# Feed-forward weights split by two DMAs instead of ScalarE and VectorE, and one square moved from GpSimd to VectorE

## The chip, the cores and the metric

The kernel runs on one core of one Trainium2 chip. The metric is the device time of one execution in microseconds, the median of three runs. Times inside an execution come from one profiled execution and are counted from its first instruction.

## What is computed

Two layers of a decoder trunk over 512 tokens of width 1024. Each layer has a token mixer (pooling, latent attention and a recurrent unit, merged by gates, then an output projection `w_out`) and after it a feed-forward block with a hidden width of 4096. Only the feed-forward block is touched by the change:

```python
h = rms_norm(x, g_ffn[l])
x = x + jnp.square(jax.nn.relu(h @ w_ff1[l])) @ w_ff2[l]
```

All arrays are float32. The kernel keeps float32 accuracy on TensorE by splitting each operand into a high and a low part (type float32r) with high + low equal to the operand, and by summing three products: high by high, high by low, low by high.

## The kernel before

Activations lie transposed: 8 blocks of 128 channels by 512 tokens. Weights lie in DRAM as chunks of 128 by 1024 floats (512 KB), contraction on partitions. A chunk serves eight 128 by 128 blocks, and each block takes part in three matmuls of 512 columns (`three`), so a chunk is used by 24 matmuls.

`chunk` (line 132) brings a chunk in: SyncE's queue loads it into one of three `raw` buffers (`load`, line 127), ScalarE rounds it into the high part `whi` (line 137), and VectorE subtracts to get the low part `wlo` (line 138). `whi` and `wlo` have two buffers each. These buffers lie in the pool `wpool`, which is open for the whole program, and all chunks of both layers pass through them in order, those of the mixer and of the feed-forward block alike.

Per layer the program opens and closes pools of SBUF in nested blocks (lines 587 to 604). The pools `mix`, `at` and `mg` hold the mixer's tiles; `mg` holds the merged activations `mgh` and `mgl`, which are the moving operands of the output projection `wo` (lines 596 to 600), the last step of the mixer. When these pools are closed, the pool `ff` (`ffp` in the code) is opened at the place where they lay. The framework's rule for such a pool, in its default form that this kernel uses, is that all its tiles wait for every user of the closed pools on whose bytes it lies. The permanent pools take some 118 KB of a partition, `mix` and `at` together some 105 KB, and `ff` 72 KB (100 KB with the change), so `ff` cannot lie beside the mixer's pools.

The feed-forward block runs over two halves of the hidden width (line 605). A half has 16 chunks of `w_ff1`, one for each block of 128 hidden channels: 24 matmuls into an accumulator `f`, then `ft` = max(f, 0) times the norm's factor on VectorE (line 618), the high part `ah` = square of `ft` on ScalarE (line 621), the float32 square of `ft` in place on GpSimd (line 622), and the low part `al` on VectorE (line 623). Then come 16 chunks of `w_ff2`, two for each of the eight output blocks, 48 matmuls into one accumulator, which VectorE adds to x (line 523). That makes 64 chunks per layer and 128 in all. The order of instructions on each engine is set by the framework's scheduler when the program is built, by its own estimate of times and by program order.

Other work of GpSimd near the block: the sum of squares of x for the norms (line 168). SyncE's queue also stores and reloads x between the layers.

Of the kernel before, what the change touches and what calls it, by code (L numbers as in the profile page):

```python
# [10 lines left out]
F32R = mybir.dt.float32r  # L11
AF = mybir.ActivationFunctionType
# [3 lines left out]
P = 128  # L16
# [17 lines left out]
HALVES = 2  # L34
HEAD = 10           # matmuls of the second half of the tokens ahead of the first half's sum of squares
SPLIT = 4           # output blocks of the first half ahead of the second half's last addition
EARLY = (0, 2, 4, 6)  # heads that a gate is computed before
LRU_N = 9           # gates ahead of the gates of the LRU
DEPTH = 4           # column blocks of gates ahead of the merge
ON_POOL = 2         # heads from here on form their q on the Pool engine  # L40
N_X, N_TMP, N_E, N_Z, N_RAW, N_W = 15, 6, 5, 6, 3, 2
N_PSUM = dict(acc=3, s=2, t=2, o=1)
FB = FF // P // HALVES

# order of the weight chunks of a layer, each [128, 1024] with the contraction on partitions
C_CKV, C_KR, C_QL, C_LRU, C_POOL = 0, 2, 3, 6, 8
# [5 lines left out]

# columns of the per-channel vectors of a layer
V_GMIX, V_GQ, V_GKV, V_PSC, V_CW, V_CB = 0, 8, 11, 13, 15, 23
# [3 lines left out]

# columns of the constants
K_COS, K_SIN, K_MASK, K_ID, K_ONE, K_ROT, K_CNT, K_INV = 0, 512, 1024, 1536, 1664, 1792, 1920, 1952  # L60
# [4 lines left out]
def trunk(ctx: ExitStack, tc, x_in, wts, vecs, consts, out):  # L65
# [11 lines left out]

    # ---- constants and per-channel vectors
    cst = const.tile([P, NCONST], F32, name="cst")
# [13 lines left out]

    # blocks of x and gates share their buffers: x waits in DRAM while the branches are computed
    def xtile(name):
# [9 lines left out]

    # ---- helpers
    def acc(name, tag="acc", bufs=None):
# [24 lines left out]
    def chunk(l, c, cols=1024, off=0):  # L132
# [6 lines left out]
        return hi, lo  # L139

    def blk(t, k):
        return t[:, k * P:(k + 1) * P]

    def dense(dst, w, acts, off=0):
        """dst[m, t] = sum_k w[k, m] * act[k, t]"""
        terms = []
        for k, (h, lo_) in enumerate(acts):
            terms += three(blk(w[0], off + k), blk(w[1], off + k), h, lo_)
        matmuls(dst, terms)

    def split(src, hi, lo, scale=None, eng=nc.vector):
        """hi + lo = src * scale, each float32r"""
        if scale is None:
            nc.scalar.copy(hi, src)
            eng.tensor_tensor(lo, src, f(hi), op=ALU.subtract)
        else:
            nc.scalar.activation(hi, src, AF.Copy, scale=scale)
            nc.vector.scalar_tensor_tensor(lo, src, scale, f(hi), op0=ALU.mult, op1=ALU.subtract)  # L158
# [12 lines left out]
    def rsqrt_mean(s, n, dst, name):  # L171
        """dst = (sum over partitions of s / n + EPS) ** -0.5 on every partition"""
        h, lo = tmp(f"nh{name}", F32R), tmp(f"nl{name}", F32R)
        split(s, h, lo)
        tot = acc(f"tot{name}", "o", 1)
        matmuls(tot, [(ones, h), (ones, lo)])
        rsqrt(tot, n, dst, name)
# [27 lines left out]
    def setup():  # L205
        nc.scalar.dma_start(vec, vecs)
        nc.vector.memset(epst, EPS)
        nc.scalar.copy(warm, epst)
        nc.vector.memset(f(ones), 1.0)
        # the first two chunks come by halves, between the first blocks of x  # L210
        raws = [wpool.tile([P, 1024], F32, tag="raw", bufs=N_RAW, name=f"raw0_{c}") for c in range(2)]
        for k in range(KB):
            nc.sync.dma_start(x[k], x_in[k])
            if k < 4:
                c, cols = k // 2, slice(512 * (k % 2), 512 * (k % 2) + 512)
                nc.sync.dma_start(raws[c][:, cols], wts[0, c, :, cols])
        for c in range(2):
            hi, lo = ready[0, c] = wtiles(0, c)
            for i in range(2):
                cols = slice(512 * i, 512 * i + 512)  # L220
                nc.scalar.copy(hi[:, cols], raws[c][:, cols])
                nc.vector.tensor_tensor(lo[:, cols], raws[c][:, cols], f(hi[:, cols]), op=ALU.subtract)
        nc.sync.dma_start(cst, consts)
# [4 lines left out]
    def setup_vectors():  # L228
        for l in range(L):
            nc.vector.tensor_scalar(hb[:, l, :], vcol(l, V_BA, 28), 0.5, None, op0=ALU.mult)  # L230
        # sp4 = 4 * softplus(-lam), with log1p(z) = 2 * atanh(z / (2 + z))
        lam = const.tile([P, L, 2], F32, name="lam")
# [31 lines left out]
    def mixer(l, mix, rstd, xs):  # L264
        """pool, latent attention and RG-LRU branches; returns their inputs to the projections"""
        ot = [tuple(mix.tile([P, S], F32R, tag="ot", bufs=8, name=f"ot{l}_{p}{c}") for c in "hl") for p in range(4)]
        us = [mix.tile([P, S], F32, name=f"u{l}_{b}") for b in range(2)]
        with ExitStack() as st:
# [27 lines left out]

            # the first projections run while the norm of x is still being found
            a0, a1 = project(C_CKV, "s"), project(C_CKV + 1, "s")
# [4 lines left out]
            zc = [latent_in(a0, "ckv", 0), latent_in(a1, "ckv", 1)]  # L303
            # columns of the stationary: high and low part of the 32 columns, twice
            raw = load(l, C_KR)
# [35 lines left out]

            # multi-scale pooling: groups of 64 channels, windows 2 4 8 16
            def pool_in(b):
# [23 lines left out]

            # the "ssq" buffers are free from the latent norms to the norm of the ffn
            pm = [tmpp.tile([P, S], F32, tag="ssq", bufs=2, name=f"pm{l}_{b}") for b in range(2)]
# [5 lines left out]

            # ---- attention
            wv = chunk(l, C_V)
            v = []
            for t in range(4):
# [8 lines left out]
                v.append(vv)  # L388
            # the blocks (j, i), i >= j, of the transposed probabilities are at 3 j + i, and zeros at 11
            pt = [at.tile([P, 13, P], F32R, name=f"pt{l}{c}") for c in "hl"]  # L390
# [4 lines left out]
            for h in range(NH):  # L395
# [3 lines left out]
                if e == 0:  # L399
# [12 lines left out]
                    dense(qn, wq, qlat)  # L412
                # q: 64 rows as they are, 32 rows times cos, 32 rows times sin
                q = tmp(f"q{l}_{h}")
# [11 lines left out]
                for i in range(4):  # L426
# [3 lines left out]
                    p = at.tile([P, S + 8], F32, tag="e", bufs=N_E, name=f"p{l}_{h}{i}")  # L430
                    # p = -scale * (s + mask), its minimum is -scale * rowmax
                    nc.vector.tensor_tensor_reduce(
# [7 lines left out]
                for i in range(4):  # L440
# [5 lines left out]
                    split(tp[:, :n, :], *dst)  # L446
                # rows 0:64 and 64:128 of o are the products with the high and the low parts of v
                o = acc(f"o{l}_{h}", "o")
# [12 lines left out]
    def pool_lru_out(l, mix, us, pm):  # L461
        w = chunk(l, C_SMALL, 768)
        res = [], []
        for b in range(2):
# [6 lines left out]
            for g, t in enumerate((tr, ti)):  # L471
                a = acc(f"ra{l}_{b}{g}")
                dense(a, w, [ly], 2 * b + g)
                nc.scalar.activation(t, a, AF.Tanh, bias=hb[:, l, 2 * g + b:2 * g + b + 1], scale=0.5)
            # a = exp(-sp4 (1 + tr));  1 - a^2 = th (1 + a^2), th = tanh(sp4 (1 + tr))
            av, th = tmp(f"av{l}_{b}"), tmp(f"th{l}_{b}")
# [47 lines left out]

    # ---- final norm, the last block of x by halves of the tokens
    halves = [slice(0, S // 2), slice(S // 2, S)]
# [14 lines left out]
    def finish(k, accs, terms):  # L541
        """the last block of x and the final norm, by halves of the tokens"""
        ones32 = cst[:, K_ONE:K_ONE + P]
# [38 lines left out]

    # ---- program
    x = [xtile(f"x{k}") for k in range(KB)]
    saved = [x_in[k] for k in range(KB)]
    setup()
    for l in range(L):
# [15 lines left out]
        with ExitStack() as st:  # L603
            ffp = st.enter_context(tc.tile_pool(name=f"ff{l}", bufs=1))
            for hf in range(HALVES):
                base = C_FF + hf * FF_STEP
                act = []
                first = acc(f"f1{l}_{hf}0")
                dense(first, chunk(l, base), xs)
                if hf == 0:  # L610
                    norm_x(f"f{l}", rstd, ssq)
                for m in range(FB):
                    a = first
                    if m:
                        a = acc(f"f1{l}_{hf}{m}")
                        dense(a, chunk(l, base + m), xs)
                    t = tmp(f"ft{l}_{hf}{m}")
                    nc.vector.scalar_tensor_tensor(t, a, 0.0, rstd, op0=ALU.max, op1=ALU.mult)  # L618
                    h = ffp.tile([P, S], F32R, tag="ah", bufs=FB + 2, name=f"ah{l}_{hf}{m}")
                    lo = ffp.tile([P, S], F32R, tag="al", bufs=FB + 2, name=f"al{l}_{hf}{m}")  # L620
                    nc.scalar.activation(h, t, AF.Square)  # L621
                    nc.gpsimd.tensor_tensor(t, t, t, op=ALU.mult)  # L622
                    nc.vector.tensor_tensor(lo, t, f(h), op=ALU.subtract)
                    act.append((h, lo))
                for j in range(KB):
                    w = [chunk(l, base + FB + 2 * j + i) for i in range(2)]
                    final = l == L - 1 and hf == HALVES - 1
# [22 lines left out]
def _blocks(w):  # L650
    """[K, M] -> [M/128, 128, K]: per block of 128 columns, k-blocks side by side"""
    k, m = w.shape
# [69 lines left out]
def _constants():  # L722
# [9 lines left out]
    c[:, K_ONE:K_ONE + P] = 1.0  # L732
    # rows: twice cos * k, twice sin * k; columns: the rotated key, and its halves swapped with a sign
    half = ROPE // 2
# [34 lines left out]
```

## Time and profile before

| | us |
|---|---|
| median of three runs | 1408.69 (1407.93 to 1408.70) |
| span of the profiled execution | 1406.1 |
| TensorE busy | 1379.1 |
| VectorE, ScalarE, GpSimd busy | 773.8, 559.7, 320.7 |

The profiled execution's span runs from its first to its last instruction; the medians of the runs are 2.6 us above it. A busy TensorE counts pipelined matmuls from start to modelled end. Issuing a DMA isn't counted as busy time of an engine.

### The profile page before, as it was taken

What the parts mean: (1) busy time and instruction counts of PE and PEld (TensorE: products, weight loads), DVE (VectorE), ACT (ScalarE), POOL (GpSimd) and SP (SyncE); (2) the same over time, 40 slices, a digit from 0 to 9 for tenths busy, and PEclk for the clock granted to TensorE, in tenths of its full rate; (3) what the DMA queues carried; (4) which work ended last, traced back from release to release, by engine and by line L of the source; (5) the groups of instructions that cost most, each with busy time, mean ns of one, the idle gap of its engine ahead of it and who ended that gap; (6) DMA issues with size and microseconds to landing.
All of it is one profiled execution on the core that took longest, in us unless ns stands there. A gap on an engine that the chain in (4) does not pass through costs nothing.

```text
span 1406.1 us, 16117 instructions
## 1 busy us (share of the span) xinstructions
PE 1379.1 (98%) x6252; PEld 1142.1 (81%) x6252; DVE 773.8 (55%) x1122; ACT 559.7 (40%) x847; POOL 320.7 (23%) x234
## 2 busy tenths in 40 slices
PE   7999999999999999999999999999999999999997
PEld 5877888888888888888887878888888888888886
DVE  8978774574544234443368887655745433344323
ACT  5457683324332112323244777632333221232322
POOL 3265101132322002211115530111232200022112
PEclk9999999999999999999999999999999999999999
DMA  5321122253332323233332212223423233333231
GB/s 200 100 79 61 57 79 100 91 155 100 94 102 92 104 90 105 90 112 113 121 104 85 72 58 73 90 90 105 150 90 105 91 104 90 105 90 105 91 103 62
DMA packets 42124, 137.38 MB, mean 98 GB/s; under 512 B 4672, under 2 KB 6848, under 8 KB 42048
## 3 DMA queue, kind: packets, MB, share of 16 engines
q1 hardware_dynamic: 41328, 135.76, 30.6%
q8 instruction: 49, 0.80, 0.2%
q10 hardware_dynamic: 720, 0.59, 0.1%
q14 instruction: 27, 0.22, 0.0%
HBM read 132.14 MB, written 4.19 MB: 97 GB/s over the span
## 4 chain that ended last, share of the span: by engine, by line
PE 91%; DVE 6%; issue 1%; ACT 1%; DMA 0%; DVEq 0%; ACTq 0%
PE f L116 50%; PE ga L116 17%; PE wo L116 6%; PE pj L116 6%; PE in L116 5%; PE s L116 2%; PE o L452 1%; DVE wlo L138 1%; PE t L444 1%; DVE q L420 1%; PE qr L116 1%; PE ka L116 1%; PE qn L116 1%; DVE qll L158 1%; DVE p L438 0%
## 5 line engine op out<-in xcount | busy, mean ns | idle before, releaser
L137 ACT CAST whi<-raw 128x1024 fp32r<-128x1024 f32 (+1 forms) x236 | 246.7, 1045 | 687.4 <-issue 381.9
L138 DVE TENSOR_TENSOR wlo<-raw,whi 128x1024 fp32r<-128x1024 f32 (+1 forms) x236 | 307.0, 1301 | 162.3 <-ACT whi L137 162.2
L116 PE MATMUL f<-al,whi 128*128 128x512 f32 (+1 forms) x528 | 202.2, 383 | 0.0
L116 PE MATMUL f<-ah,whi 128*128 128x512 f32 (+1 forms) x528 | 202.0, 383 | 0.0
L116 PE MATMUL f<-ah,wlo 128*128 128x512 f32 (+1 forms) x528 | 202.0, 383 | 0.0
L116 PE MATMUL f<-xhf,whi 128*128 128x512 f32 x512 | 199.2, 389 | 0.0
L116 PE MATMUL f<-xlf,whi 128*128 128x512 f32 x512 | 199.2, 389 | 0.0
L116 PE MATMUL f<-xhf,wlo 128*128 128x512 f32 x512 | 199.2, 389 | 0.0
L622 POOL TENSOR_TENSOR ft<-ft 128x512 f32<-128x512 f32 x64 | 94.4, 1477 | 426.9 <-ACT ah L621 426.9
L116 PE MATMUL ga<-xhm,whi 128*128 128x512 f32 x384 | 151.3, 394 | 2.5 <-ACT q L415 2.5
L116 PE MATMUL ga<-xhm,wlo 128*128 128x512 f32 x384 | 151.2, 394 | 0.0
L116 PE MATMUL ga<-xlm,whi 128*128 128x512 f32 x384 | 150.6, 392 | 0.0
L116 PEld LDWEIGHTS f<-al,whi 128*128 128x128 f32 x528 | 99.2, 188 | 19.5
L116 PEld LDWEIGHTS f<-ah,wlo 128*128 128x128 f32 x528 | 99.2, 188 | 19.4
L116 PEld LDWEIGHTS f<-ah,whi 128*128 128x128 f32 x528 | 99.2, 188 | 19.2
L116 PEld LDWEIGHTS f<-xlf,whi 128*128 128x128 f32 x512 | 96.1, 188 | 20.0
L116 PEld LDWEIGHTS f<-xhf,wlo 128*128 128x128 f32 x512 | 96.1, 188 | 20.0
L116 PEld LDWEIGHTS f<-xhf,whi 128*128 128x128 f32 x512 | 96.1, 188 | 19.9
L618 DVE SCALAR_TENSOR_TENSOR ft<-f,rstdf 128x512 f32<-128x512 f32 x64 | 44.1, 692 | 102.1 <-PE f L116 102.0
L116 PEld LDWEIGHTS ga<-xhm,whi 128*128 128x128 f32 x384 | 72.2, 188 | 17.6 <-ACT q L415 3.0
L116 PEld LDWEIGHTS ga<-xlm,whi 128*128 128x128 f32 x384 | 72.2, 188 | 14.3
L116 PEld LDWEIGHTS ga<-xhm,wlo 128*128 128x128 f32 x384 | 72.2, 188 | 14.3
(366 smaller groups left out, 2119.8 us busy)
## 6 DMA issues: line engine op xcount, KB each, us to landing
raw<-wts SPq DMA_DIRECT2D x232, 512.0 KB, 3.5
x<-x_in SPq DMA_DIRECT2D x8, 256.0 KB, 5.4
xr<-x_in SPq DMA_DIRECT2D x8, 256.0 KB, 2.9
saved<-xr SPq DMA_DIRECT2D x8, 256.0 KB, 2.0
xr<-saved SPq DMA_DIRECT2D x8, 256.0 KB, 3.1
out<-xr SPq DMA_DIRECT2D x12, 128.0 KB, 1.8
raw<-wts SPq DMA_DIRECT2D x4, 320.0 KB, 2.9
raw<-wts SPq DMA_DIRECT2D x4, 256.0 KB, 4.5
```

What stands on the lines that cost most here:

```text
L116: ins = nc.tensor.matmul(dst, lhsT=a, rhs=b, start=(start and i == 0), stop=(stop and i == n - 1))
L137: nc.scalar.copy(hi[:, :cols], raw[:, :cols])
L138: nc.vector.tensor_tensor(lo[:, :cols], raw[:, :cols], f(hi[:, :cols]), op=ALU.subtract)
L158: nc.vector.scalar_tensor_tensor(lo, src, scale, f(hi), op0=ALU.mult, op1=ALU.subtract)
L420: eng.tensor_tensor(q[o:o + ROPE], qr[src], table[src], op=ALU.mult)
L444: nc.tensor.transpose(tp[:, j, :], blk(probs[i], j), ident)
L452: nc.tensor.matmul(o[:, q0 * P:], lhsT=v[j][:, h, :, :], rhs=pt[c][:, 3 * j + q0:3 * j + 4, :], start=(j == 0 and c == 0), stop=(j == 3 an ...
L618: nc.vector.scalar_tensor_tensor(t, a, 0.0, rstd, op0=ALU.max, op1=ALU.mult)
L622: nc.gpsimd.tensor_tensor(t, t, t, op=ALU.mult)
```

## The change

Feed-forward chunks no longer pass through `raw`, `whi` and `wlo`. A new function takes two tiles of the pool `ff`, with four buffers each (`fwh` and `fwl`). A DMA issued by GpSimd loads the chunk into `fwh`, casting from float32 to float32r. ScalarE writes its negative into `fwl`. A second DMA issued by GpSimd loads the same chunk from DRAM once more and adds it to what stands in `fwl`, which leaves the low part. The square of `ft` moves from GpSimd to VectorE, and `ah` and `al` go from 18 to 17 buffers. Comments and docstrings are dropped as well, which is left out here.

```diff
+N_FW = 4
+    def chunk_by_dma(l, c, pool):
+        hi, lo = (pool.tile([P, 1024], F32R, tag=t, bufs=N_FW, name=f"{t}{l}_{c}") for t in ("fwh", "fwl"))
+        nc.gpsimd.dma_start(hi, wts[l, c])
+        nc.scalar.activation(lo, f(hi), AF.Copy, scale=-1.0)
+        nc.gpsimd.dma_start(lo, wts[l, c], accum_op=ALU.add)
+        return hi, lo
...
-                dense(first, chunk(l, base), xs)
+                dense(first, chunk_by_dma(l, base, ffp), xs)
...
-                        dense(a, chunk(l, base + m), xs)
+                        dense(a, chunk_by_dma(l, base + m, ffp), xs)
...
-                    h = ffp.tile([P, S], F32R, tag="ah", bufs=FB + 2, name=f"ah{l}_{hf}{m}")
-                    lo = ffp.tile([P, S], F32R, tag="al", bufs=FB + 2, name=f"al{l}_{hf}{m}")
+                    h = ffp.tile([P, S], F32R, tag="ah", bufs=FB + 1, name=f"ah{l}_{hf}{m}")
+                    lo = ffp.tile([P, S], F32R, tag="al", bufs=FB + 1, name=f"al{l}_{hf}{m}")
                     nc.scalar.activation(h, t, AF.Square)
-                    nc.gpsimd.tensor_tensor(t, t, t, op=ALU.mult)
+                    nc.vector.tensor_tensor(t, t, t, op=ALU.mult)
                     nc.vector.tensor_tensor(lo, t, f(h), op=ALU.subtract)
...
-                    w = [chunk(l, base + FB + 2 * j + i) for i in range(2)]
+                    w = [chunk_by_dma(l, base + FB + 2 * j + i, ffp) for i in range(2)]
```

## Rows read from the trace of the kernel before

**Rows 1.** The page's parts 1 and 2: busy time by engine, and forty slices.

```profile
PE 1379.1 (98%) x6252; PEld 1142.1 (81%) x6252; DVE 773.8 (55%) x1122; ACT 559.7 (40%) x847; POOL 320.7 (23%) x234
PE   7999999999999999999999999999999999999997
```

**Rows 2.** The chain that ended last, in order of time: start us, length us, what.

```profile
311.69 43.52 PE wo L116 x192
355.21 8.61 PE f L116 x38
364.96 338.87 PE f L116 x1495
1001.30 43.52 PE wo L116 x192
1044.82 8.61 PE f L116 x38
```

**Rows 3.** Stretches: length, then busy time and count by engine, clock, DMA share, GB/s.

```profile
core 0: us, PE busy (x) PEld busy (x) DVE busy (x) ACT busy (x) POOL busy (x), PEclk, DMA share, GB/s
364.90:703.80 338.90, 338.90 (x1497) 280.62 (x1496) 137.59 (x152) 92.08 (x112) 58.12 (x38) 1.00 0.33 104
720.00:800.00 80.00, 77.96 (x351) 63.63 (x350) 68.08 (x98) 42.08 (x69) 34.87 (x27) 1.00 0.28 85
1054.50:1389.00 334.50, 334.50 (x1504) 278.10 (x1503) 132.16 (x145) 92.14 (x111) 57.20 (x38) 1.00 0.30 93
```

**Rows 4.** Groups of layer 0's feed-forward stretch: busy us, mean ns, idle before, releaser.

```profile
L137 ACT CAST whi<-raw 128x1024 fp32r<-128x1024 f32 x63 | 66.4, 1054 | 244.0 <-issue 138.8 <-PE f L116 105.3
L138 DVE TENSOR_TENSOR wlo<-raw,whi 128x1024 fp32r<-128x1024 f32 x63 | 77.2, 1225 | 71.8 <-ACT whi L137 71.8
L623 DVE TENSOR_TENSOR al<-ft,ah 128x512 fp32r<-128x512 f32 x32 | 23.0, 723 | 27.1 <-POOL ft L622 27.1
L622 POOL TENSOR_TENSOR ft<-ft 128x512 f32<-128x512 f32 x32 | 47.4, 1482 | 213.3 <-ACT ah L621 213.3
```

**Rows 5.** DMAs of the same stretch: queue, packets, MB, share; then issue to landing.

```profile
q1 hardware_dynamic: 10073, 34.87, 32.4%
raw<-wts SPq DMA_DIRECT2D x63, 512.0 KB, 3.5
```

**Rows 6.** Line 129 in 640 to 660 us, durations min/median/max in ns, of the issue.

```profile
L129 SPq DMA_DIRECT2D raw<-wts x4: 328/328/328, 640.7 to 657.1; - x4
```

**Rows 7.** Timeline of TensorE at the two ends of layer 0's and 1's `wo`.

```profile
311.30 0.39 PE L116 MATMUL pj<-ot_3h,wlo 128*128 128x512 f32 x1
...
1044.43 0.39 PE L116 MATMUL wo<-mgh,wlo 128*128 128x512 f32 x1
1044.66 0.39 PE L116 MATMUL f<-xhf,whi 128*128 128x512 f32 x1
```

**Rows 8.** Timelines of GpSimd and of VectorE where layer 1's mixer pools open.

```profile
703.89 0.11 POOL L345 MEMSET pz<- 128x8 f32 x1 [7.01 <-PE f L116]
...
703.86 0.69 DVE L523 TENSOR_TENSOR xr<-xr,f 128x512 f32<-128x512 f32 x1 [3.31 <-PE f L116]
704.50 0.08 DVE L333 MEMSET lz<- 128x8 f32 x2
704.55 0.17 DVE L392 MEMSET pt1h<- 128x128 f32 x1
```

**Rows 9.** TensorE's granted clock: stretches at the end, then matmuls of the start.

```profile
1396.00:1398.00 2.00, 0.70 (x2) 0.30 (x2) 0.82 (x3) 1.63 (x4) 0.00 (x0) 1.00 0.76 257
1398.00:1400.00 2.00, 0.00 (x0) 0.00 (x0) 1.77 (x5) 0.09 (x1) 0.58 (x1) 0.80 0.23 77
1400.00:1402.00 2.00, 0.00 (x0) 0.00 (x0) 2.00 (x3) 0.00 (x0) 2.00 (x3) 0.50 0.54 189
...
13.68 0.79 PE L116 MATMUL in<-xhm,wlo 128*128 128x512 f32 x1 [0.59 <-DVE wlo L222]
14.27 0.63 PE L116 MATMUL in<-xhm,whi 128*128 128x512 f32 x1
14.70 0.63 PE L116 MATMUL in<-xlm,whi 128*128 128x512 f32 x1
16.83 0.39 PE L116 MATMUL in<-xhm,whi 128*128 128x512 f32 x1
17.06 0.39 PE L116 MATMUL in<-xlm,whi 128*128 128x512 f32 x1
```

**Rows 10.** What SyncE's queue waited for: us in total, times, longest.

```profile
SPq L129 <- DVE wlo L138: 1026.3, 212, 10.5
```

## Prediction

> **What bounds the kernel now.** I read the busy shares first: TensorE is busy for 1379.1 of 1406.1 us, and its only lighter slices are the first and the last [rows 1]. Then the chain that ended last: the feed-forward blocks are long unbroken pieces of matmuls, 338.87 us for 1495 of them in layer 0, so one every 0.2267 us, and a chunk of 24 takes 5.44 us [rows 2]. Then the stretches: from 364.9 to 703.8 us TensorE is busy for all of 338.90 us, at the full clock, and in layer 1 for all of 334.50 us, while VectorE, ScalarE and GpSimd are busy for 137.6, 92.1 and 58.1 us of the first one [rows 3]. The reader is to see that in the block which the change touches no other engine sets the pace, and that there is no idle time of TensorE in it that a lighter VectorE or GpSimd could give back. Nor does the block wait at its door: the output projection `wo` ends at 355.21 us and the first feed-forward matmul starts at 355.21 us, and the same at 1044.82 us in layer 1 [rows 2]. The weights for it were converted during `wo`, because `whi` and `wlo` are always there, and SyncE's loads wait for a buffer (1026.3 us in 212 waits), not for the memory [rows 10].
>
> **What the change removes.** Per chunk it removes VectorE's subtraction of 1.225 us; ScalarE's rounding of 1.054 us becomes a negation of the same shape, which I take at the same time [rows 4]. GpSimd's square of 1.48 us becomes one on VectorE, whose nearest row is the subtraction of 0.72 us [rows 4]. So VectorE is at 64 x 1.225 - 32 x 0.72, some 55 us less per layer, and `al` is ready some 0.8 us earlier. All of it lies beside a TensorE that is busy all the time, so it is worth nothing. If that cover were gone (TensorE waiting for weights), it would still be worth nothing, since VectorE has slack. The 17th instead of the 18th buffer of `ah` and `al` costs nothing either: the second half needs its first new buffer when TensorE begins that half, and by then the first half's matmuls, in TensorE's own order, are done with theirs.
>
> **What it adds, in the steady state.** A chunk now needs two DMAs. The queue moved 34.87 MB in 32.4% of 338.9 us, which is 318 GB/s while it moves, or 1.65 us for 512 KB [rows 5]. The casting DMA I take at that. The adding DMA has to read what stands in `fwl` as well; I take it at twice, 3.30 us (low end 1.65, as a plain load; high end 6.6, if it runs at half speed). Together 4.95 us per 5.44 us: it fits, with little to spare. In time: a load took 3.5 us from issue to landing [rows 5]. From a free buffer to a ready chunk it is then 3.5 for the cast, 1.05 for the negation and 0.2 for the two handovers, and 3.5 + 1.65 for the addition, 9.9 us. Four buffers give 3 x 5.44 = 16.3 us. So the steady state holds with 6.4 us in reserve, at a cost of nothing. No row shows a DMA issued by GpSimd; the bounds of one issue are 0.33 us, SyncE's row [rows 6], and 1.5 us, about a whole GpSimd instruction on 512 columns [rows 4].
>
> The Trainium skill (DMA: Bandwidth & Descriptors, Latency and other measured facts) states about 1 us to the first byte for a DMA issued by GpSimd against 0.6 us for one from SyncE. By that page each DMA here would land 0.4 us later, and the sum below would grow by 0.8 us per layer; no run before shows it. The same page (Rules for kernel authors) says that an accumulating DMA reads its destination and writes it later. That speaks for the second read that I charge; without it the sum would shrink by 1.65 us per layer.
>
> **What it adds at the door of each block.** This is the term that counts. `fwh` and `fwl` are tiles of the pool `ff`, which lies where the mixer's pools lay, so the first cast has to wait for their last user, and that is the last matmul of `wo` at 355.2 us. The rows show that such a wait is real: when layer 1's mixer pools open where `ff` lay, a memset of GpSimd, which reads nothing, comes only at 703.89 us, after 7.01 us idle, released by the last feed-forward matmul; VectorE sat idle for 3.31 us up to 703.86 us, and its three memsets come after that too [rows 8]. In the kernel before, nothing at this door needs a tile of `ff` before the first accumulator is full, so the wait is hidden. After the change TensorE needs both parts of the first chunk. Its wait, from 355.2 us:
>
> - cast of chunk 0, issue to landing: 3.5 us [rows 5];
> - negation and two handovers: 1.05 + 0.2 = 1.25 us;
> - addition: 3.5 + 1.65 = 5.15 us;
> - queueing: casts 1 to 3 are issued right behind cast 0. Four casts of 1.65 us, from 1.85 us after the issue (3.5 - 1.65), are through after 8.45 us; the addition could start to move at 3.5 + 1.25 + 1.85 = 6.6 us, so it waits for 1.85 us;
> - less the two matmuls with the high part that run before the low part is needed: 2 x 0.2267 = 0.45 us.
>
> That is 11.3 us without work. TensorE's clock falls in such a gap: at the end of the program it was granted in full up to 1398 us, at 0.80 over the next 2 us and at 0.50 (1.2 GHz) after that, with the last matmul before 1398 us [rows 9]. At the start of the program seven matmuls from 13.68 to 16.83 us go at some 0.43 us each until the pitch is 0.23 us [rows 9]. I charge seven times 0.2 = 1.4 us. Behind that the next chunks follow: each addition takes 3.30 us of the DMA engines, the matmuls of a chunk 5.44 us. Sum per layer 12.7 us, two layers 25.4 us: a span of 1406.1 + 25.4 = 1431.5, and with the 2.6 us by which the median stands above the profiled span, **1434.1 us**. The bounds of this term per layer: 3.5 + 1.25 + 3.5 - 0.45 = 7.8 us, with no second read, no queueing and no slow clock; and some 21 us, if the addition moves at half speed (3.3 us more), each of two issues takes 1.5 us and the clock costs 3 us. That makes 1424 to 1451 us.
>
> What is late next: the mixer's first chunk in layer 1 no longer stands in one ring behind feed-forward chunks, so its conversion can be done earlier. The idle time of TensorE after that door is 80 - 77.96 = 2.0 us [rows 3], and that bounds the gain.
>
> **The rivals.**
>
> *No stall at the door (not slower).* If a tile of `ff` waited only for the users of its own bytes, `fwh` and `fwl`, the first tiles of the pool, would lie where `ot` and the latents lay, last read at 311.30 us [rows 7]. Then the 9.9 us chain would fit easily into the 43.5 us of `wo`. It decides if the first cast is issued before 345 us. The time would be 1408.7, or up to 2.0 us less by the door of layer 1's mixer: 1406.7 to 1408.7. Against it stand the framework's rule and the late memsets [rows 8].
>
> *GpSimd's order becomes the bound.* GpSimd works in order. If the scheduler put the addition of chunk c ahead of the cast of chunk c+1, that cast would be queued behind a wait for cast, landing and negation. One turn would then be 3.5 + 1.25 plus two issues: 5.4 us at 0.33 us per issue, no loss, and 7.75 us at 1.5 us, 2.3 us too long for each chunk. At 1 us per issue it is 6.75 us, 1.3 us too long; over some 120 chunks that is 157 us, a total of about 1590 us. For it: a landing plus a negation comes so close to 5.44 us that the order is a toss-up. Against it: with four buffers the next cast is free to go as soon as TensorE has left a buffer, which on a wait-free estimate is about when the addition is ready.
>
> *The DMA engines become the bound.* With the cast and the addition both at half speed, a chunk takes 3.3 + 6.6 = 9.9 us instead of 5.44 us, 4.5 us for each of some 124 chunks: about 1990 us. With the addition alone at half speed it is 8.25 us and about 1780 us. No row speaks for it but the 91% share worked out above, and none excludes it.
>
> **How the numbers follow.** The door stall with a steady state that holds: 0.48, 1434 us, own range 1424 to 1451. GpSimd's order or a longer chain that costs something in each chunk: 0.25, spread from 1450 to 1640. DMA engines too slow: 0.12, from 1600 up. No stall: 0.10, 1406.7 to 1408.7. Half a stall, where the first casts do get away early: 0.05, 1412 to 1424. From 1416 to 1640 us the first two cases, some of the third and most of the last lie inside, about 8 in 10. A measurement of this kernel tells 0.2%, 2.8 us, from no change. Faster by more than that needs more than the 2.0 us that the mixer's door holds: 0.03. The same: the rest of the no-stall case, 0.07. Slower: 0.90.
>
> **What would show it right or wrong.** Right: two idle gaps of TensorE, of 8 to 20 us each, just behind the last `wo` matmul of each layer, released by a DMA into `fwl`; the granted clock below 1.00 right after them; no idle time from then to the end of each block; the first cast on GpSimd's queue at the end of `wo`. Wrong in the door: a cast issued while `wo` is running. Wrong in the steady state: gaps once per chunk, at a DMA share near 1.0 (the DMA engines) or with GpSimd's queue waiting for ScalarE most of the time (the order). The forecast as a whole falls if the time is below 1420 or above 1455 us.

## The result, and the profile after

The changed kernel takes 1556.03 us (median; 1555.30 to 1559.03) against 1408.54 us before: a ratio of 1.105, 95% interval 1.1035 to 1.1064, or 147.5 us more. The forecast was 1434 us, with a range from 1416 to 1640 us. So the direction was right, the size was not, and the time that came out lies in the spread of the second rival, "GpSimd's order becomes the bound" (1450 to 1640 us).

First the stretches of the changed kernel, one for each mixer and each feed-forward block, in that order. Columns: stretch, length, busy time of TensorE, its weight loads, VectorE, ScalarE and GpSimd with counts, granted clock, DMA share, GB/s.

```profile
0.00:355.60 355.60, 342.23 (x1560) 281.56 (x1560) 251.38 (x419) 187.18 (x315) 102.87 (x80) 1.00 0.32 103
355.60:781.00 425.40, 375.44 (x1542) 299.06 (x1541) 84.87 (x126) 97.64 (x117) 101.64 (x136) 0.95 0.69 164
781.00:1121.90 340.90, 336.68 (x1560) 279.06 (x1558) 233.39 (x379) 173.06 (x291) 92.82 (x70) 1.00 0.27 85
1121.90:1554.80 432.90, 374.30 (x1594) 301.69 (x1594) 87.02 (x135) 101.22 (x124) 106.22 (x141) 0.95 0.68 160
```

The mixers are as they were (`wo` ended at 355.21 us before [rows 2]). The two feed-forward blocks hold the whole loss: 425.40 us instead of the 348.6 us from 355.2 to 703.8 us, and 432.90 instead of 361.3. In [rows 3] TensorE was busy without a gap at the full clock; now it is idle for 50.0 us of the first block (425.40 - 375.44) and needs 26.8 us more busy time for the same matmuls, at a mean granted clock of 0.95. GpSimd and ScalarE are busy for a quarter of the time, and the DMA engines for 0.69 of it: nothing that works is full.

Who waits, over the whole program (engine, line, what it waits for: us in total, times, longest):

```profile
POOL fwl L147 <- ACT fwl L146: 592.8, 122, 9.5
ACT fwl L146 <- DMA fwh<-wts: 389.6, 72, 8.7
PE f L117 <- DMA fwl<-wts: 86.8, 42, 3.5
POOL fwh L145 <- PE f L117: 19.7, 9, 6.3
```

The first line is the answer. GpSimd, which issues both DMAs, stands for 592.8 us in front of additions whose negation isn't done. It hardly ever waits for a free buffer (9 times), which is what it should be doing in a block that TensorE bounds. TensorE waits 42 times for a low part, about once in three chunks. GpSimd's timeline in the middle of the block shows why (start, length, engine, line, operation, count, idle time before and its releaser; L145 is the cast, L147 the addition):

```profile
469.74 0.90 POOL L145 DMA_DIRECT2D fwh<-wts  x1
478.58 0.88 POOL L147 DMA_DIRECT2D fwl<-wts  x1 [7.94 <-ACT fwl L146]
479.19 1.39 POOL L145 DMA_DIRECT2D fwh<-wts  x2
486.99 0.88 POOL L147 DMA_DIRECT2D fwl<-wts  x1 [6.42 <-ACT fwl L146]
488.28 0.89 POOL L147 DMA_DIRECT2D fwl<-wts  x1 [0.40 <-ACT fwl L146]
488.83 0.91 POOL L145 DMA_DIRECT2D fwh<-wts  x1
497.77 0.87 POOL L147 DMA_DIRECT2D fwl<-wts  x1 [8.04 <-ACT fwl L146]
```

Two turns alternate: one cast and its own addition, then two casts and their two additions. Each turn ends at an addition that stands right behind the casts and waits for the very cast just issued to land and be negated. The next cast stands behind it on the queue although its buffer is free. The two turns take three chunks through in 19.19 us (478.58 to 497.77), 6.40 us each, where TensorE needs 5.44. Over 128 chunks that is 123 us.

The length of a turn is mostly the cast's landing. The DMAs from 400 to 760 us (count, size, median us from issue to landing):

```profile
fwh<-wts POOLq DMA_DIRECT2D x56, 512.0 KB, 6.9
fwl<-wts POOLq DMA_DIRECT2D x55, 512.0 KB, 5.5
```

A cast lands after 6.9 us here, not after the 3.5 us that the prediction took from SyncE's loads; in these rows it is issued 0.6 us behind an addition (478.58 and 479.19 us).

The rest is the door. TensorE around the end of layer 0's `wo`:

```profile
355.46 0.39 PE L117 MATMUL wo<-mgh,wlo 128*128 128x512 f32 x1
360.37 0.77 PE L117 MATMUL f<-xhf,fwh 128*128 128x512 f32 x1 [4.52 <-DMA fwh<-wts]
...
368.73 0.79 PE L117 MATMUL f<-xhf,fwl 128*128 128x512 f32 x1 [3.22 <-DMA fwl<-wts]
```

The first matmul with a low part starts 13.0 us after `wo` (355.69 to 368.73), in layer 1 after 11.5 us, and it takes 0.79 us instead of 0.39 [rows 7]: the clock is at its lower level. GpSimd's side of it:

```profile
356.18 2.38 POOL L145 DMA_DIRECT2D fwh<-wts  x4 [1.80 <-PE wo L117]
...
361.67 0.92 POOL L147 DMA_DIRECT2D fwl<-wts  x1 [1.82 <-ACT fwl L146]
```

The first four casts are released by the last `wo` matmul, as the prediction said.

### The profile page after: what moved, and what is told of

The parts are those of the page before. It is cut to its first block, busy times and chain, and to the rows that moved or that the text cites. A ratio compares the mean times of both kernels' runs of the same rounds, so it can differ in the third digit from the quotient of the medians.

```text
span 1554.8 us, 16092 instructions
## 1 busy us (share of the span) xinstructions
PE 1428.7 (92%) x6252; PEld 1161.4 (75%) x6252; DVE 656.7 (42%) x1058; ACT 559.1 (36%) x847; POOL 403.6 (26%) x426
## 4 chain that ended last, share of the span: by engine, by line
PE 24%; issue 16%; DMA 7%; POOL 4%; DVE 3%; ACT 2%; DVEq 0%; POOLq 0%; ACTq 0%
PE ga L117 8%; PE f L117 5%; DMA fwh<-wts 5%; PE wo L117 3%; PE pj L117 3%; PE in L117 3%; DMA fwl<-wts 2%; POOL fwh L145 2%; POOL fwl L147 2%; ACT fwl L146 1%; PE s L117 1%; DVE wlo L139 1%; PE o L461 0%; PE t L453 0%; POOL ssqm L177 0%
## 5 line engine op out<-in xcount | busy, mean ns | idle before, releaser
L146 ACT ACTIVATE fwl<-fwh 128x1024 fp32r<-128x1024 f32 x128 | 135.4, 1058 | 585.6 <-DMA fwh<-wts 389.6
L147 POOL DMA_DIRECT2D fwl<-wts x128 | 113.0, 883 | 597.5 <-ACT fwl L146 592.8
L117 PE MATMUL f<-ah,fwl 128*128 128x512 f32 (+1 forms) x528 | 211.8, 401 | 44.8 <-DMA fwl<-wts 44.8
L117 PE MATMUL f<-xhf,fwl 128*128 128x512 f32 x512 | 207.9, 407 | 42.2 <-DMA fwl<-wts 42.0
L117 PE MATMUL f<-xhf,fwh 128*128 128x512 f32 x512 | 206.7, 404 | 10.2 <-DMA fwh<-wts 10.0
L117 PE MATMUL f<-al,fwh 128*128 128x512 f32 (+1 forms) x528 | 207.9, 394 | 1.0 <-DVE al L632 1.0
L117 PE MATMUL f<-ah,fwh 128*128 128x512 f32 (+1 forms) x528 | 208.5, 395 | 0.0
L117 PE MATMUL f<-xlf,fwh 128*128 128x512 f32 x512 | 205.8, 402 | 0.0
L138 ACT CAST whi<-raw 128x1024 fp32r<-128x1024 f32 (+2 forms) x108 | 111.7, 1034 | 196.8 <-issue 121.2
L139 DVE TENSOR_TENSOR wlo<-raw,whi 128x1024 fp32r<-128x1024 f32 (+2 forms) x108 | 150.2, 1391 | 19.1 <-ACT whi L138 18.7
L117 PEld LDWEIGHTS f<-xhf,fwh 128*128 128x128 f32 x512 | 100.4, 196 | 32.9 <-issue 12.7
L145 POOL DMA_DIRECT2D fwh<-wts x128 | 95.2, 786 | 24.7 <-PE f L117 19.7
```

The lines of the kernel that those rows point to most:

```text
L117: ins = nc.tensor.matmul(dst, lhsT=a, rhs=b, start=(start and i == 0), stop=(stop and i == n - 1))
L138: nc.scalar.copy(hi[:, :cols], raw[:, :cols])
L139: nc.vector.tensor_tensor(lo[:, :cols], raw[:, :cols], f(hi[:, :cols]), op=ALU.subtract)
L145: nc.gpsimd.dma_start(hi, wts[l, c])
L146: nc.scalar.activation(lo, f(hi), AF.Copy, scale=-1.0)
L147: nc.gpsimd.dma_start(lo, wts[l, c], accum_op=ALU.add)
```

## The experiments

Theory: GpSimd's queue, in the order in which the scheduler built it, costs some 120 us, and the door of the two blocks some 27 us. Rivals: the DMA engines or the memory are too slow for two transfers per chunk; the square on VectorE makes the low parts late.

### The order on GpSimd's queue

All of the change is kept, but each cast is put ahead of the addition of the chunk before it.

```diff
+        last = min(c + 1, NCH - 1)
+        for n in range(c, last + 1):
+            if (l, n) not in issued:
+                cast(l, n, pool)
...
-        nc.gpsimd.dma_start(lo, wts[l, c], accum_op=ALU.add)
+        with tc.issue_after(issued[l, last][1]):
+            nc.gpsimd.dma_start(lo, wts[l, c], accum_op=ALU.add)
```

> The changed kernel with GpSimd's queue put in the order cast of chunk c+1, then addition of chunk c, throughout. Theory A (GpSimd's queue order): in the changed kernel the queue stands 592.8 us in additions that wait for ScalarE's negation, with casts behind them whose buffers are free. With one cast always ahead, two chunks share one landing plus negation of about 8 us plus the issues of 0.9 and 0.6 us, so a chunk needs about 4.8 us, below TensorE's 5.44 us. The gaps per chunk go, the wait at the start of each block (some 13 us) stays: about 1435 us. Rival B (the DMA engines or their latency set the pace, whatever the order): nothing changes, 1545 to 1560 us.

Measured: 1436.60 us (1435.55 to 1438.91), ratio 1.0200, interval 1.0184 to 1.0215. The stretch from 400 to 760 us, columns as above:

```profile
400.00:760.00 360.00, 360.00 (x1590) 298.07 (x1589) 100.32 (x143) 102.12 (x124) 95.93 (x126) 1.00 0.83 181
```

The same two lines of the waits, and a piece of GpSimd's timeline (here L147 is the cast and L158 the addition):

```profile
POOL fwh L147 <- PE f L117: 402.4, 120, 10.0
...
POOL fwl L158 <- ACT fwl L156: 90.6, 100, 3.9
```

```profile
470.60 0.55 POOL L147 DMA_DIRECT2D fwh<-wts  x1 [3.17 <-PE f L117]
471.50 0.87 POOL L158 DMA_DIRECT2D fwl<-wts  x1 [0.35 <-issue]
476.04 0.55 POOL L147 DMA_DIRECT2D fwh<-wts  x1 [3.67 <-PE f L117]
477.34 0.89 POOL L158 DMA_DIRECT2D fwl<-wts  x1 [0.75 <-ACT fwl L156]
```

Not one instruction is added or taken away, and 119.4 of the 147.5 us are gone. TensorE is busy for 360.00 of 360 us. GpSimd's waits have changed over from ScalarE (592.8 to 90.6 us) to TensorE (19.7 to 402.4 us): it waits for free buffers, and TensorE waits for nothing. The DMA engines are busier than in the changed kernel (0.83 against 0.69; from 720 us on the stretch is already layer 1's mixer, and from 400 to 700 us the share is 0.93) and hold back nobody, so they were not the bound.

### The square back on GpSimd

In the changed kernel t*t goes back from VectorE to GpSimd.

```diff
-                    nc.vector.tensor_tensor(t, t, t, op=ALU.mult)
+                    nc.gpsimd.tensor_tensor(t, t, t, op=ALU.mult)
```

> The changed kernel with one part undone: t*t is on GpSimd again (32 squares of some 1.5 us per layer, in the first half-steps only). Theory A (GpSimd's queue, in order, sets the pace of the feed-forward block in the changed kernel): what is added to that queue is added to the time, unless it falls into its waits for ScalarE; 0 to 47 us per layer, so 1556 to 1650 us, and most likely 1575. Rival (the DMA engines or the memory set the pace): the square moves nothing, 1553 to 1559 us.

Measured: 1551.69 us (1548.35 to 1552.28), no time added, some 4 us less. That is below the theory's 1556 to 1650 us and just below the rival's 1553 to 1559 us, so this run doesn't tell the two apart. The theory in the form "what is added to that queue is added to the time" fell. What stood in its place is in the waits of this run:

```profile
POOL fwl L147 <- ACT fwl L146: 499.3, 102, 8.3
```

64 squares of 1.48 us [rows 4] are 94.7 us, and GpSimd's wait shrank by 93.5 us (592.8 to 499.3). The work fell into the waits. That fits a queue whose pace is set by the place of its waits and not by the amount of work on it; what shows it is the first experiment.

### The square alone

The kernel before, with only t*t on VectorE.

> The kernel before with the square of ft moved from GpSimd to VectorE and nothing else. The prediction's step: worth nothing, since TensorE is busy all through the blocks: 1408.5 us, within 1 us. A rival would be that VectorE, which also makes the low parts of the weights here, is late for TensorE: over 1412 us.

Measured: 1409.00 us (1408.00 to 1410.14), ratio 1.0000, interval 0.9991 to 1.0009. That part of the change is worth nothing, as the prediction had it.

### Each DMA alone

First only the high part by a casting DMA; the low part is a subtraction on VectorE from the chunk as SyncE loads it.

```diff
+        raw = load(l, c)
         nc.gpsimd.dma_start(hi, wts[l, c])
-        nc.scalar.activation(lo, f(hi), AF.Copy, scale=-1.0)
-        nc.gpsimd.dma_start(lo, wts[l, c], accum_op=ALU.add)
+        nc.vector.tensor_tensor(lo, raw, f(hi), op=ALU.subtract)
```

> Only the high part comes by the casting DMA; SyncE loads the chunk as before and VectorE subtracts for the low part, into fwl. GpSimd's queue then holds casts alone and waits for no negation. Theory A (queue order): no loss per chunk; at the start of each block the cast of 4.1 us and the subtraction of 1.2 us, less the two matmuls, and the slow clock: 6 to 7 us per layer, about 1421 us. Rival B (the casting DMA itself is too slow, 6.8 us to landing against 5.44 us per chunk): 1500 us or more.

Then only the low part by the adding DMA; ScalarE rounds and negates.

```diff
+        raw = load(l, c)
-        nc.gpsimd.dma_start(hi, wts[l, c])
+        nc.scalar.copy(hi, raw)
         nc.scalar.activation(lo, f(hi), AF.Copy, scale=-1.0)
         nc.gpsimd.dma_start(lo, wts[l, c], accum_op=ALU.add)
```

> Only the low part comes by the adding DMA; SyncE loads the chunk, ScalarE makes the high part and the negative. GpSimd's queue then holds additions alone. Theory A: a waiting addition holds up no cast, so no loss per chunk; at the start of each block the rounding and the negation of 1.05 us each and the addition of 5.6 us, less the two matmuls, and the slow clock: 8 to 9 us per layer, about 1425 us. Rival B (the adding DMA itself is too slow): 1500 us or more.

Measured: the cast alone 1422.90 us (1421.98 to 1423.92), the addition alone 1434.87 us (1433.00 to 1436.04). In both, TensorE is busy for 300.00 us from 400 to 700 us: neither DMA costs anything in the steady state, and what is lost lies at the doors. With the cast alone that is 7.2 us per layer (a landing of 4.04 us and one subtraction). With the addition alone it is 13.2 us, 10 us in all more than I expected: the addition stood on GpSimd behind the last addition of the sum of squares (L177), and TensorE waited for the norm as well (9.4 us in two waits for `nhf`):

```profile
359.86 1.27 POOL L177 TENSOR_TENSOR ssqf<-ssqf,sqf 128x512 f32<-128x512 f32 x1 [6.26 <-ACT sqf L176]
361.07 2.81 POOL L147 DMA_DIRECT2D fwl<-wts  x3
```

The two runs also give each transfer's price, since GpSimd's DMA queue holds 128 transfers of one kind (packets, MB, share of 16 engines). The cast, in a span of 1420.3 us, and the addition, in 1431.2 us:

```profile
q0 software_dynamic: 18432, 67.12, 15.3%
```

```profile
q0 software_dynamic: 18432, 67.12, 28.5%
```

0.153 x 1420.3 / 128 = 1.70 us for a cast and 0.285 x 1431.2 / 128 = 3.19 us for an addition, 4.89 us for both. The prediction had taken 1.65, 3.30 and 4.95.

### Three buffers instead of four

The run with the order changed, and N_FW = 3.

> The kernel with the queue in order (one cast ahead) and three buffers instead of four. There a cast took 5.1 us and an addition 6.9 us to land, with the negation and the issues some 14 us from a free buffer to a ready chunk; three buffers give 2 x 5.44 = 10.9 us. So the time should rise by 0.6 us (with the shorter landings of less loaded queues) to 1.8 us per chunk, to 1500 to 1650 us. If the reserve were as large as the prediction had it (9.9 us needed), it would stay at 1437 us.

Measured: 1555.64 us (1552.18 and 1559.11), 119 us more than with four, some 0.95 us for each of 125 chunks. So in this order the reserve of four buffers is less than one chunk's 5.44 us, not 6.4. It is not a clean measure of the landings: in this order the addition of a chunk also waits behind a cast that waits for a buffer, and with three buffers only one chunk's time is left from there, against a landing of 6.3 us. How much of the 0.95 us each of the two makes wasn't separated. The waits of this run are a warning for the reading above:

```profile
POOL fwh L147 <- PE f L117: 590.6, 122, 10.6
...
PE f L117 <- DMA fwl<-wts: 88.2, 76, 2.7
```

GpSimd waits for free buffers even more than with four (590.6 against 402.4 us), and yet the block is late: here the buffers come free too late. That nothing is lost is seen in TensorE's own waits, not in GpSimd's.

### The door: which bar holds the first casts

Expected from the prediction: the pool's rule holds the first cast until the end of `wo`. First the rule is relaxed, in the changed kernel and in the one with the order changed.

```diff
-            ffp = st.enter_context(tc.tile_pool(name=f"ff{l}", bufs=1))
+            ffp = st.enter_context(tc.tile_pool(name=f"ff{l}", bufs=1, reuse_waits="tile"))
```

> The changed kernel with the pool ff waiting only for users of its tiles' own bytes, so that the first four casts may be issued while the output projection runs. Both theories: the wait at the start of each block goes (TensorE began the first low-part matmul 13.1 us after the end of wo in layer 0, 11.5 us in layer 1), the loss per chunk stays: 1556 - 25 = about 1531 us. If the rival that said the pool's rule costs nothing were right, it would stay at 1556 us.

> Both edits: the queue order with one cast ahead, and the pool that waits by bytes. Theory A: nothing of the loss is left, 1408 to 1412 us. Rival B: 1525 to 1535 us, as with the pool's edit alone.

Measured: 1551.81 us (1548.62 to 1559.34) and 1431.60 us (1429.18 to 1432.81): 4 and 5 us better than without it, not 25; the first of the two differences is smaller than the spread of its own runs. GpSimd's timeline of the second one:

```profile
353.89 1.78 POOL L188 TENSOR_TENSOR ssqf<-ssqf,sqf 128x512 f32<-128x512 f32 x1 [3.66 <-ACT sqf L187]
355.62 2.37 POOL L147 DMA_DIRECT2D fwh<-wts  x4
```

The casts wait for nothing now and still go out at 355.6 us: the scheduler had put them on the queue behind the sums of squares, each of which waits for a chunk of `wo`. A second bar stood where the first was taken away. Next, the first four casts are put ahead of the sums of squares.

```diff
+            for c in range(N_FW):
+                cast(l, C_FF + c, ffp)
             xs = gained(l, V_GFF, f"f{l}")
-            rstd, ssq = rstd_tile(f"f{l}"), sumsq_x(f"f{l}")
+            with tc.issue_after(issued[l, C_FF + N_FW - 1][1]):
+                rstd, ssq = rstd_tile(f"f{l}"), sumsq_x(f"f{l}")
```

> Both edits of the run before, and GpSimd's queue is made to hold the first four casts of a block ahead of the additions for the sum of squares of x (line 177), behind which they stood until 355.6 us. Theory (the wait at the start of each block has two bars, the pool's rule and GpSimd's queue order; only both together free it): the casts go out at about 311 us, when the last matmul on ot has run, the first chunks are ready during wo, and nothing is left of the loss: 1408 to 1413 us. Rival (the additions for the norm, now behind casts and additions of weights, come late, or early transfers collide with wo's loads): 1420 us or more.

Measured: 1431.89 us (1431.31 to 1434.47), nothing gained. GpSimd, then ScalarE:

```profile
313.60 2.37 POOL L147 DMA_DIRECT2D fwh<-wts  x4 [3.40 <-PE pj L117]
...
359.79 0.92 POOL L158 DMA_DIRECT2D fwl<-wts  x1 [31.44 <-ACT fwl L156]
```

```profile
356.87 1.05 ACT L138 CAST whi<-raw 128x1024 fp32r<-128x1024 f32 x1 [3.25 <-issue]
357.82 0.72 ACT L177 ACTIVATE xhf<-xr,vec 128x512 fp32r<-128x512 f32 x1
358.44 1.99 ACT L156 ACTIVATE fwl<-fwh 128x1024 fp32r<-128x1024 f32 x2
```

The casts are 42 us earlier, and the addition isn't: the negation stands on ScalarE behind work that follows the last chunks of `wo`. That is a third bar. The next run puts the casts, negations and additions of the first three chunks ahead of the norm on both engines, and the fifth chunk's cast behind the sums of squares.

```diff
+            for c in range(N_FW - 1):
+                chunk_by_dma(l, C_FF + c, ffp)
+            _, neg, add = made[l, C_FF + N_FW - 2]
+            with tc.issue_after(neg), tc.issue_after(add):
+                xs = gained(l, V_GFF, f"f{l}")
+                rstd, ssq = rstd_tile(f"f{l}"), sumsq_x(f"f{l}")
```

> Everything of the change stays; the pool waits by tile, each cast stands ahead of the addition of the chunk before it, and the casts, negations and additions of a block's first three chunks stand on GpSimd and ScalarE ahead of the norm's sums of squares and ahead of whi and xhf of the last output-projection chunks. Theory A (the stall at the door has three bars one behind the other, the pool's rule, GpSimd's order and ScalarE's order, so that freeing one or two of them moves nothing): all three are free now, TensorE goes from wo to f without a gap over 2 us, and the time is 1408 to 1413 us, level with the kernel before. Rival (the stall has a further cause that the order doesn't remove, such as the moving operand xhf or the weights of the last wo chunks coming late): a gap of 5 us or more stays at each door, and the time is 1420 us or more.

Measured: 1437.90 us (1436.45 to 1439.41), 6 us worse than the run before, and the theory's number missed. ScalarE:

```profile
357.31 1.04 ACT L138 CAST whi<-raw 128x1024 fp32r<-128x1024 f32 x1 [4.38 <-PE wo L117]
358.26 2.94 ACT L162 ACTIVATE fwl<-fwh 128x1024 fp32r<-128x1024 f32 x3
361.12 4.99 ACT L184 ACTIVATE xhf<-xr,vec 128x512 fp32r<-128x512 f32 x8
```

The negations now stand ahead of `xhf` but still behind the last rounding of `whi`, which waits for a matmul of `wo`; and all of `xhf` has become late too. So this run had not removed the third bar. The next one goes round ScalarE: GpSimd, idle from 316 us on, negates the first three chunks, and `gained` is left where it was.

```diff
+        if C_FF <= c < C_FF + N_FW - 1:
+            neg = nc.gpsimd.tensor_scalar(lo, f(hi), -1.0, None, op0=ALU.mult).ins
+        else:
+            neg = nc.scalar.activation(lo, f(hi), AF.Copy, scale=-1.0).ins
```

> Like the run with three bars, but the negations of a block's first three chunks are made by GpSimd instead of ScalarE, and whi, xhf and xlf are left where the changed kernel has them; only the norm's sums of squares on GpSimd stand behind the three additions. In the run with three bars the negations still came at 358.26 us, because they stood on ScalarE behind the rounding of the last chunk loaded during wo, which waits for a matmul of wo until 357.31 us; GpSimd has nothing else to do from 316 to 355 us. Theory A (the third bar is ScalarE's order, and that run didn't remove it): the first additions are issued by about 335 us, both parts of the first chunk are there before wo ends, the gap of TensorE at each door is under 3 us, and the time is 1408 to 1414 us. Rival 1 (the negation or the addition waits for the end of wo itself, because fwl lies on bytes that wo still reads): the additions are issued only after 355 us and 1425 to 1435 us come out. Rival 2 (the norm comes late instead, because its sums of squares now stand behind the additions): a gap at the first ft and 1415 to 1425 us.

Measured: 1423.52 us (1422.12 to 1423.79), above the theory's 1408 to 1414 us and in the range of rival 2. The additions go out at 326.56 us, and the first `f` matmul follows the last `wo` matmul without a gap. One gap is left in each block; TensorE and ScalarE there:

```profile
373.73 0.39 PE L117 MATMUL f<-xhf,fwl 128*128 128x512 f32 x1
378.71 0.79 PE L117 MATMUL f<-xhf,fwh 128*128 128x512 f32 x1 [4.59 <-DVE ft L652]
```

```profile
368.12 1.06 ACT L165 ACTIVATE fwl<-fwh 128x1024 fp32r<-128x1024 f32 x1 [5.87 <-DMA fwh<-wts]
...
372.12 0.69 ACT L211 ACTIVATE nyf<-totf,epst 128x512 f32<-128x512 f32 x1 [1.64 <-PE totf L117]
374.37 1.06 ACT L165 ACTIVATE fwl<-fwh 128x1024 fp32r<-128x1024 f32 x1 [1.56 <-DMA fwh<-wts]
375.33 0.61 ACT L212 ACTIVATE ntf<-nyf 128x512 f32<-128x512 f32 x1
```

The norm's factor is late, not because of the sums of squares (rival 2 as I had put it) but because its step `ntf` stands behind a negation that waits for a landing: a fourth bar, of the same kind. The last run puts `totf` earlier on TensorE and the fifth chunk's negation behind `ntf`.

```diff
+            with tc.issue_after(norm["ntf"]) if c == C_FF + N_FW else ExitStack():
+                neg = nc.scalar.activation(lo, f(hi), AF.Copy, scale=-1.0).ins
...
+                            matmuls(a, ts[:6], stop=False)
+                            with tc.issue_after(norm["tot"]):
+                                matmuls(a, ts[6:], start=False)
```

> Like the run in which GpSimd makes the first three negations, which left one gap of TensorE in each block, 4.6 us long at 373.9 us, before the matmul that waits for ft. In that run the norm's factor came late: the two matmuls of totf stood at 370.79 and 371.69 us, and its ntf on ScalarE at 375.33 us behind a negation that waited for a cast to land. Here the totf matmuls stand in the second chunk of the block, and the negation of the fifth chunk stands behind ntf. Theory A (the rest of the loss is the fourth bar, the norm's steps queued behind a negation): ntf is done by about 366 us, the gap is gone, and the time is 1408 to 1412 us, within 0.3% of the kernel before. Rival (the fifth chunk's low part comes late now, because its negation and addition are put back): a gap of 3 to 6 us at the fifth chunk, and 1415 to 1424 us.

Measured: 1412.06 us (1410.39 to 1413.01), ratio 1.0019, interval 1.0010 to 1.0029. TensorE's one remaining wait for something of this block, then two pieces of the chain that ended last (start, length, what):

```profile
PE f L117 <- DVE ft L663: 1.4, 1, 1.4
```

```profile
314.07 43.52 PE wo L117 x192
357.59 12.41 PE f L117 x54
```

The gap in layer 0 is gone and that in layer 1 is 1.4 us. `totf` came only at 369.83 us, later than I had meant; it was early enough. Which of the two edits closed the gap wasn't separated. By the medians 3.2 us of the loss are left. The profiled execution is 4.8 us longer than the one before (spans of 1410.9 and 1406.1 us), and 2.4 us of that are there before `wo` begins (314.07 against 311.69 [rows 2]): in the first 20 us TensorE runs at the lower clock until 18.7 us instead of 16.8 [rows 9], ahead of everything the change touches. That part isn't shown to be the change's, since in the run with the square alone, whose time is level, `wo` began at 313.49 us. From the start of `wo` to the end the execution is 2.4 us longer, of which 1.4 are the gap in layer 1.

No version beats the kernel before. With all bars away the change comes within 0.2% of it, which is what [rows 3] said: there was no idle time of TensorE in the block to win.

## Why the prediction was right or wrong

- *What bounds the kernel*: right. TensorE had no gap in the block; the best form of the change comes out within 0.2%, and the square on VectorE is worth 0.0%.
- *Steady state*: this is the step that failed: "the steady state holds with 6.4 us in reserve, at a cost of nothing". It lost 119 us. The sum added up landings as if each cast were issued when its buffer came free. That holds only if nothing waiting stands ahead of it on GpSimd's queue, and in the built order an addition stood there that waits for a cast and a negation. The sizes alone were not the cause: engine time per chunk was 4.89 us (predicted 4.95), the chain with the changed kernel's own landings would be 6.9 + 1.05 + 0.2 + 5.5 = 13.7 us (an estimate), still under the 16.3 us of four buffers, and with the same DMAs in another order the cost is nothing, as forecast. Nor was the order alone: with the forecast landing of 3.5 us the two turns would take 19.19 - 2 x 3.4 = 12.4 us (an estimate) for three chunks, under TensorE's 16.3 us. The loss needs both, the order and a landing of 6.9 us in each turn.
- *The reserve*: also too large, which by itself would have cost nothing with four buffers. Landings in the steady state were 5.1 us for a cast and 6.9 us for an addition in the run with the order changed, against 3.5 and 5.15 us.
- *The rival "GpSimd's order"*: its mechanism was right. That its price was near, 6.75 us per chunk at 1 us per issue against 6.40 us measured, is luck: it counted one turn for each chunk with a landing of 3.5 us, and the trace has two turns for three chunks with a landing of 6.9 us and issues of 0.55 us and 0.88 us. The two errors offset each other. It had 0.25. The reason against it, "with four buffers the next cast is free to go as soon as TensorE has left a buffer, which on a wait-free estimate is about when the addition is ready", speaks only of when the two are ready, and that is the toss-up of the sentence before it. It was no reason to give the hopeful order twice the chance. The sign that the prediction named, "gaps once per chunk [...] with GpSimd's queue waiting for ScalarE most of the time", is what the trace shows, at one gap in three chunks: GpSimd waits for ScalarE for 592.8 us of the two blocks' 858.3 us.
- *The door*: right in size. Predicted 12.7 us per layer; with the order mended the loss is 28.1 us, 14.0 per layer. Term by term in that run: the cast landed in 4.09 and 3.98 us (predicted 3.5), the negation took 1.06 (1.05), the addition 7.54 and 5.61 us with its queueing (5.15 + 1.85). Two smaller terms were off and nearly cancel. In layer 0 TensorE did eight matmuls within the wait (six with the high part, two of the norm), not two, which is worth 1.4 us more. And the clock stayed at its lower level for thirteen matmuls behind the wait, from 370.84 to 376.55 us at some 0.43 us each; that is about 2.8 us (an estimate: 5.71 - 13 x 0.2267) instead of the 1.4 us charged. The granted clock was 0.64 from 355 to 370 us in the changed kernel.
- *The door's cause*: only one of four. The prediction knew the pool's rule. (Of its rows for that rule only GpSimd's memset bears it out; VectorE's 3.31 us of idle time ended at a sum that reads `f` itself [rows 8].) Behind it stood GpSimd's sums of squares, ScalarE's roundings, and the norm's last steps, each late enough to keep the loss. Its rival "no stall at the door", which hung on the pool's rule alone, would have been wrong for that reason: with the rule relaxed 23 of 28 us stay.
- *What is late next*: no gain came. Layer 1's mixer took 340.90 us, against 341.00 us before (703.8 to 1044.8 us).
- *The DMA engines as a bound*: excluded, at a share of 0.93 TensorE is still full.

## What to carry to other kernels

An engine that issues DMAs in order holds every later transfer behind one that waits, as GpSimd did here (7.94 us ahead of the addition at 478.58 us, with two casts right behind it); so when a chunk needs two dependent transfers from one queue, write the order out (the next chunk's first transfer ahead of this chunk's second) instead of leaving it to a scheduler, and before pricing transfers by their landings ask what stands ahead of each on its queue. In the waits, an issuing engine that waits for a producer while buffers are free is the place to look. One that waits for a free buffer is not for that reason healthy (402.4 us with four buffers and no loss in the block, 590.6 us with three and 119 us lost): whether anything is lost is read from TensorE's waits. A stall at the door of a block can have several bars one behind the other, and freeing one moves little until the next is freed (5 us of 28 for the first one here): follow the first late instruction on each queue in turn.

## What was unexpected of the hardware

- At the doors a cast issued by GpSimd landed in some 4 us (4.09 and 3.98 us with the order changed, 4.04 us with the cast alone), about 0.5 us more than SyncE's load of the same size in the block [rows 5]. The Trainium skill (DMA: Bandwidth & Descriptors, Latency and other measured facts) gives about 1 us to the first byte for a DMA issued by GpSimd and 0.6 us for one from SyncE, 0.4 us apart; the trace, which has landings and not first bytes, agrees roughly.
- An addition held the DMA engines for 3.19 us per 512 KB, a cast for 1.70 us. That the accumulating transfer also reads its destination, as the same page says (Rules for kernel authors), agrees with a price of 1.9 times.
- Short waits cost clock as well: with one gap of some 2 us in three chunks the mean granted clock of the whole block was 0.95. It is at the lower level (1.2 GHz) behind some gaps and not behind others: after 2.67 us of idle time up to 492.44 us seven matmuls went at some 0.43 us each, after 2.30 us up to 472.91 us they went at 0.23 us. The 26.8 us more of busy time include these stretches and the slow start of the block; how much of the 119 us they make wasn't separated, and the run with the order changed gets the clock and the gaps back at once.
